# A decoder step on one core: rows of 320 floats for the normed inputs and the gate*up outputs, placed by address

## The chip, the core and the metric

The kernel runs on one core of a Trainium2 chip. The metric is device time in microseconds for one execution. Three executions of the kernel before took 1245.39 to 1247.6 us, with a median of 1246.92 us.

The core has five engines, each with its own queue, and they meet only at semaphores: PE (TensorE, matrix products), DVE (VectorE), ACT (ScalarE), POOL (GpSimd) and SP (SyncE, which here only issues DMAs). Tiles lie in SBUF, which has 128 partitions; a tile takes the same range of byte addresses in each of them. PE writes its sums into PSUM. A matrix product is two instructions on PE: LDWEIGHTS (PEld in the profile) reads the stationary operand from SBUF, and MATMUL (PE in the profile) streams the moving operand from SBUF past it.

## The reference

One inference step of a two-layer decoder for 256 prompt tokens and 8 times 4 sample tokens, 288 tokens in all, with a model width of 1024 and an FFN width of 2816. Each layer is a mixer between two half-step SwiGLU FFNs; the mixer of layer 0 is a short gated convolution, that of layer 1 a sparse attention with three branches.

```
xp = xp + 0.5 * swiglu(rmsnorm(xp, norm_ffa[i]), w_ffa_gu[i], w_ffa_down[i])
...
xp = xp + 0.5 * swiglu(rmsnorm(xp, norm_ffb[i]), w_ffb_gu[i], w_ffb_down[i])

def swiglu(x, w_gu, w_down):
    g, u = jnp.split(x @ w_gu, 2, axis=-1)
    return (jax.nn.silu(g) * u) @ w_down
```

The four FFNs, the projections into and out of the convolution and those into and out of the attention are products of the 288 tokens with some 170 MB of weights in float32. These products are what the change touches.

## The kernel before

All activations lie turned: 128 channels on the partitions, the 288 tokens along the free axis. The normed input of a layer is eight such rows (KD = 8), the gated hidden values of half an FFN are ten or twelve.

**Three products for one.** The float32 products run in a fast format with fewer bits (float32r). So that nothing is lost, both operands are split into a high and a low part, and three of the four cross products are summed in PSUM: high by high, low by high, high by low. For the weights, `Weights.high` (L223) writes `whi` by a copy on ACT and `Weights.low` (L245) writes `wlo` by a subtraction on DVE, each 128 x 1024 floats from a `raw` tile that a DMA has filled; there are four buffers of each. For the activations the pairs are `xh`, `xl` (the normed input, written by `gated_hi` and `gated_lo`) and `Ah`, `Al` (the gated values, written at L552 and L553 in `ffn` and in `parts` of `conv_mixer`).

**The stream on PE.** `product` (L467) goes over the rows k and issues, for each, three matmuls through `mm` (L303): `ah[k]` past `hi[k]`, `al[k]` past `hi[k]`, `ah[k]` past `lo[k]`. The stationary operand is 128 columns of 4 bytes, so 512 bytes in each partition; the moving operand is one row of 288 floats, 1152 bytes. Every matmul has a LDWEIGHTS of its own, also where the weights are those of the matmul ahead. While one matmul streams, PE already loads the weights of the next: beside `ah[k]` past `hi[k]` runs the load of `hi[k]` again, beside `al[k]` past `hi[k]` that of `lo[k]`, and beside `ah[k]` past `lo[k]` that of `hi[k+1]`. `products2` (L476) does the same for two outputs at once. There are 7800 such matmuls.

**The rows.** `xh` and `xl` are tiles of 8 x 288 floats in a pool that lives through the whole kernel; `attention_out` (L1513) replaces them, for the rest of layer 1, by a second pair of the same names in another pool. `Ah` and `Al` are tiles of 12 x 288 floats, made by `pair` (L526). A row of 288 floats is 1152 bytes, four and a half times 256, so every second row starts 128 bytes further on modulo 256. `product` takes its operands from these tiles by index and knows no addresses. In the built program the tiles start, modulo 256 bytes, at

| tile | row k even | row k odd | distance to the weights' start, modulo 256 |
|---|---|---|---|
| `whi`, `wlo` (each of the 8 pieces of 512 bytes) | 224 | 224 | |
| `xh`, `xl`, first pair | 64 | 192 | 96 and 224 |
| `xh`, `xl`, second pair (from `attention_out` on) | 0 | 128 | 32 and 160 |
| `Ah`, `Al` | 0 | 128 | 32 and 160 |

**Order.** The source order sets the order on each engine outside the attention; inside it a planner (`Plan`) does. Weights come in through SP's queue in chunks of up to 1 MB into four `raw` buffers, and are split two units ahead of their use.

Of the kernel before, what the change touches and what calls it, by code (L numbers as in the profile page):

```python
# [9 lines left out]
F32R = mybir.dt.float32r  # L10
# [6 lines left out]
P = 128  # L17
D = 1024
KD = D // P
# [6 lines left out]
N = NP + NS  # L26
# [39 lines left out]
EARLY = ("POOL", "DVE", "DVE")  # L66

V_FFA, V_PE, V_MIX, V_FFB, V_FIN, V_CONV = 0, 16, 32, 48, 64, 72


def weight_chunks():
# [200 lines left out]
def tile_step(ctx, tc, x_turned, vectors, state_turned, cmp_pages, sel_pages, cache_win, win_pages, page_table,  # L272
# [4 lines left out]
    const = ctx.enter_context(tc.tile_pool(name="const", bufs=1))  # L277
# [15 lines left out]
    def mmb():  # L293
        return bank("mm")
# [7 lines left out]
    def mm(out, lhsT, rhs, start, stop):  # L302
        nc.tensor.matmul(out, lhsT, rhs, start=start, stop=stop, skip_group_check=True)  # L303
# [3 lines left out]
    work = ctx.enter_context(ExitStack())  # L307
# [64 lines left out]
    for _ in range(4):  # L372
        c = W.chunk()
# [4 lines left out]
    plan_ffn()  # L378


    xh = const.tile([P, KD, N], F32R, name="xh")
    xl = const.tile([P, KD, N], F32R, name="xl")
    ss = const.tile([P, N], F32, name="ss")
    normed = [xh, xl]

# [20 lines left out]
    def gated(d, v):  # L406

        gated_hi(d, v)
        gated_lo(d, v)
        squares(d)  # L410
# [56 lines left out]
    def product(p, ah, al, k0, nk, start, stop, lower=None):  # L467
        hi, lo = W.next(lower)
        o = p[:hi.shape[2], :N]
        for k in range(nk):  # L470
            s, e = start and k == 0, stop and k == nk - 1
            mm(o, hi[:, k], ah[:, k0 + k], s, False)
            mm(o, hi[:, k], al[:, k0 + k], False, False)
            mm(o, lo[:, k], ah[:, k0 + k], False, e)
# [18 lines left out]
    def tick(cost):  # L493

        due = [w for w in waiting if w[0] <= 1]
        waiting[:] = [w for w in waiting if w[0] > 1]
        for w in waiting:
            w[0] -= 1
        for _, f in due:
            f()  # L500
        fill.step(cost, 0 if fill.hold else 1)
# [22 lines left out]
    fill = Fill()  # L524

    def pair(work, name, n):  # L526
        return (work.tile([P, n, N], F32R, name=name + "h", bufs=1), work.tile([P, n, N], F32R, name=name + "l", bufs=1))

    def passing(d):

# [4 lines left out]

    def ffn(work, after, begin=None):
        Ah, Al = pair(work, "A", 12)
        factor = []

# [48 lines left out]

    def conv_mixer(work, v_next):
        Ah, Al = pair(work, "A", 12)  # L590
        ust = work.tile([P, KD, 18], F32, name="ust", bufs=1)
        rB = None
# [919 lines left out]

    def attention_out(work, v_next):  # L1513

        normed[:] = pair(work, "x", KD)
        ps = [mmb(), mmb()]
        us = [W.next(), W.next()]
        for n, (part, x) in enumerate(((0, xh), (0, xl), (1, xh))):
            for p, u in zip(ps, us):
                for k in range(KD):  # L1520
                    mm(p[:, :N], u[part][:, k], x[:, k], n == 0 and k == 0, n == 2 and k == KD - 1)
        for d in range(KD):
            if d < 2:
                p = ps[d]
            else:
                p = mmb()
                product(p, xh, xl, 0, KD, True, True)
            nc.vector.tensor_add(xT[:, d], p[:, :N], xT[:, d])
            gated(d, v_next)
            tick(3.0)  # L1530
# [20 lines left out]
    with psum_banks(mm=4, tr=2, acc=2), tc.tile_pool(name="ffn1", bufs=2) as work:  # L1551
        attention_out(work, V_FFB + KD)
        for b in range(NB):
            later(1 + 4 * b, lambda b=b: nc.gpsimd.dma_start(win_s[b], cache_win[0, b, NT:]))
        ffn(work, lambda d: last(work, d))
        final_out(work)
# [57 lines left out]
```

## Time and profile before

| | |
|---|---|
| median of three runs | 1246.92 us (1245.39 to 1247.6) |
| profiled execution, its own time | 1246.98 us |
| span of its trace, first to last instruction | 1245.2 us |
| granted TensorE clock, mean | 0.998 |
| MATMULs in the trace | 10047, of which 7800 are the split products |
| busy: PE, DVE, ACT, POOL | 99%, 58%, 46%, 19% of the span |
| DMA | 262 MB, mean 210 GB/s |

Times are microseconds from the first instruction unless marked ns. A group of instructions is a line of kernel.py with an engine, an operation and the names of its tiles, `mm<-xh,whi` being a product of `xh` and `whi` into PSUM tile `mm`. MATMULs overlap in the trace: the recorded time of one runs from its start to the modelled end of its results, so it is longer than the distance from one start to the next. That distance is called the **step** below. It is read from the chain that ended last, which gives the start, the length and the count of an unbroken run of matmuls: length by count is the mean step.

### The profile page before, as it was taken

Reading aid. Unit: us, or ns where it says so; the run is one execution under the profiler, and the core shown is the slowest. Engines: PE = TensorE matmul, PEld = TensorE weight load, DVE = VectorE, ACT = ScalarE, POOL = GpSimd, SP = SyncE. Lnnn points to the kernel's source line nnn. Section 1 sums busy time; section 2 is a strip of 40 time slices with the busy share of each in tenths; the row PEclk is TensorE's granted clock in tenths of the full one; section 3 lists DMA queues with packets and bytes.
Section 4 is the critical chain, followed back from the end, with each engine's and each line's share of the span. In section 5 each row is a group of like instructions: output and inputs, shape, how many; then the busy total and the mean of one; then the engine's idle time right before and its main releaser. Section 6 shows DMA issues by size and latency. Waiting matters only on the chain.

```text
span 1245.2 us, 25757 instructions
## 1 busy us (share of the span) xinstructions
PE 1227.8 (99%) x10047; PEld 1162.6 (93%) x10047; DVE 726.3 (58%) x1363; ACT 571.2 (46%) x1011; POOL 241.2 (19%) x237
## 2 busy tenths in 40 slices
PE   9999999999999999999999999999999999999997
PEld 8999999999999999999899999999866699999997
DVE  6663555666765545556564455677568566654554
ACT  6443344533544334335343344544377655433444
POOL 0260121221322201212120012130022222200211
PEclk9999999999999999999999999999999999999999
DMA  7764655756566466546563453496699857565422
GB/s 278 257 216 173 236 171 185 254 186 218 189 213 211 155 206 233 198 151 232 197 237 117 176 174 115 165 339 219 232 362 331 291 209 302 191 249 203 165 101 78
DMA packets 89066, 262.00 MB, mean 210 GB/s; under 512 B 9937, under 2 KB 43090, under 8 KB 73714
## 3 DMA queue, kind: packets, MB, share of 16 engines
q1 hardware_dynamic: 87922, 249.66, 57.0%
q0 software_dynamic: 256, 8.32, 1.7%
q10 hardware_dynamic: 768, 2.38, 0.5%
q8 instruction: 79, 1.29, 0.4%
q14 instruction: 41, 0.34, 0.1%
HBM read 257.31 MB, written 11.35 MB: 216 GB/s over the span
## 4 chain that ended last, share of the span: by engine, by line
PE 91%; DVE 3%; ACT 3%; DMA 2%; issue 1%; SPq 0%; POOL 0%; DVEq 0%; ACTq 0%
PE mm L303 82%; PE tr L303 5%; PE acc L303 3%; PE tr L334 1%; DMA early<-in_sel_pages_dram 1%; DVE wlo L247 1%; ACT S L1211 1%; DMA raw<-in_w_nsa_out_dram 0%; SPq L1008 0%; ACT L534 0%; ACT whi L238 0%; DMA wlo<-in_sel_pages_dram 0%; DMA raw<-in_w_ffa_gu_dram 0%; DVE xT L583 0%; ACT S L1367 0%
## 5 line engine op out<-in xcount | busy, mean ns | idle before, releaser
L303 PE MATMUL mm<-xh,whi 128*128 128x288 f32 x1832 | 543.3, 298 | 3.0 <-DVE xl L1476 1.1
L303 PE MATMUL mm<-xh,wlo 128*128 128x288 f32 x1832 | 539.9, 297 | 0.0
L303 PE MATMUL mm<-xl,whi 128*128 128x288 f32 x1832 | 532.8, 293 | 0.0
L247 DVE TENSOR_TENSOR wlo<-raw,whi 128x1024 fp32r<-128x1024 f32 (+2 forms) x361 | 407.8, 1143 | 94.3 <-ACT whi L238 91.5
L238 ACT ACTIVATE whi<-raw 128x1024 fp32r<-128x1024 f32 (+2 forms) x365 | 343.3, 952 | 100.3 <-PE mm L303 92.9
L303 PEld LDWEIGHTS mm<-xh,whi 128*128 128x128 f32 x1832 | 342.9, 188 | 8.8 <-issue 4.2
L303 PEld LDWEIGHTS mm<-xl,whi 128*128 128x128 f32 x1832 | 346.8, 190 | 0.3
L303 PEld LDWEIGHTS mm<-xh,wlo 128*128 128x128 f32 x1832 | 341.8, 187 | 0.6 <-DVE wlo L247 0.4
L303 PE MATMUL mm<-Ah,wlo 128*128 128x288 f32 x768 | 228.6, 298 | 1.0 <-DVE wlo L247 0.9
L303 PE MATMUL mm<-Ah,whi 128*128 128x288 f32 x768 | 227.9, 297 | 0.0
L303 PE MATMUL mm<-Al,whi 128*128 128x288 f32 x768 | 227.2, 296 | 0.0
L549 POOL TENSOR_TENSOR a<-s,t 128x288 f32<-128x288 f32 x80 | 110.3, 1379 | 517.8 <-DVE t L547 405.5
L303 PEld LDWEIGHTS mm<-Ah,wlo 128*128 128x128 f32 x768 | 144.2, 188 | 2.3 <-DVE wlo L247 2.1
L303 PEld LDWEIGHTS mm<-Ah,whi 128*128 128x128 f32 x768 | 145.0, 189 | 0.6 <-issue 0.4
L303 PEld LDWEIGHTS mm<-Al,whi 128*128 128x128 f32 x768 | 144.6, 188 | 0.0
L552 ACT ACTIVATE Ah<-a 128x288 fp32r<-128x288 f32 x88 | 39.1, 445 | 163.4 <-POOL a L549 150.1
L545 ACT ACTIVATE s<-t 128x288 f32<-128x288 f32 x88 | 39.1, 445 | 156.4 <-DVE t L543 156.3
L547 DVE TENSOR_TENSOR t<-mm,rB 128x288 f32<-128x288 f32 x88 | 40.2, 457 | 115.1 <-PE mm L303 115.1
L583 DVE SCALAR_TENSOR_TENSOR xT<-mm,xT 128x288 f32<-128x288 f32 x64 | 29.2, 456 | 90.1 <-PE mm L303 89.9
L553 DVE TENSOR_TENSOR Al<-a,Ah 128x288 fp32r<-128x288 f32 x88 | 40.8, 463 | 65.9 <-ACT Ah L552 65.9
L303 PE MATMUL tr<-cp,W 128*64 128x256 f32 x512 | 58.8, 382 | 0.0
L387 ACT ACTIVATE xh<-xT,vecT 128x288 fp32r<-128x288 f32 x48 | 25.2, 534 | 62.0 <-DVE xT L583 41.1
(283 smaller groups left out, 847.1 us busy)
## 6 DMA issues: line engine op xcount, KB each, us to landing
raw<-in_w_ffb_gu_dram SPq DMA_DIRECT2D x44, 1024.0 KB, 5.2
raw<-in_w_ffa_gu_dram SPq DMA_DIRECT2D x42, 1024.0 KB, 5.3
cp<-in_cmp_pages_dram SPq DMA_DIRECT2D x256, 128.0 KB, 4.3
early<-in_sel_pages_dram SPq DMA_DIRECT2D x56, 256.0 KB, 5.8
raw<-in_w_ffa_down_dram SPq DMA_DIRECT2D x16, 768.0 KB, 4.5
raw<-in_w_conv_in_dram SPq DMA_DIRECT2D x12, 1024.0 KB, 5.1
raw<-in_w_ffb_down_dram SPq DMA_DIRECT2D x16, 768.0 KB, 5.9
raw<-in_sel_pages_dram SPq DMA_DIRECT2D x48, 256.0 KB, 5.0
```

What stands on the lines that cost most here:

```text
L238: self.nc.scalar.activation(parts[0], v, AF.Copy)
L247: (lower or self.nc.vector).tensor_sub(parts[1], v, parts[0])
L303: nc.tensor.matmul(out, lhsT, rhs, start=start, stop=stop, skip_group_check=True)
L334: nc.tensor.transpose(out, in_, ident[:k, :k])
L387: nc.scalar.activation(normed[0][:, d], xT[:, d], AF.Copy, scale=vecT[:, v + d:v + d + 1])
L545: nc.scalar.activation(s1, t1, AF.Silu)
L547: nc.vector.tensor_mul(t2, pu[:, :N], rB)
L549: (nc.vector if last else nc.gpsimd).tensor_mul(a, s1, t2)
L552: nc.scalar.activation(Ah[:, f], a, AF.Copy)
L553: nc.vector.tensor_sub(Al[:, f], a, Ah[:, f])
L583: nc.vector.scalar_tensor_tensor(xT[:, d], py[:, :N], 0.5, xT[:, d], op0=OP.mult, op1=OP.add)
L1211: nc.scalar.activation(o, o, AF.Exp, scale=-1.0, bias=x, accum_out=e)
```

## The change

The two tiles of a pair are now made by a new function `rows`. A row takes 320 floats (1280 bytes, five times 256), of which the first 288 are used, so that all rows of a tile start at the same address modulo 256. `SKIP` leaves 0, 16 or 56 floats free ahead of the first row, and `BEHIND` leaves some free behind the last, so that whatever lies next starts where it should. The second pair of normed inputs is now called `zh`, `zl`, so that `SKIP` can treat it on its own.

```
+ROW = 320
+SKIP = dict(xh=0, xl=16, Ah=56, Al=16, zh=56, zl=16)
+BEHIND = dict(xl=8, zl=56)

-    xh = const.tile([P, KD, N], F32R, name="xh")
-    xl = const.tile([P, KD, N], F32R, name="xl")
+    def rows(pool, name, n, **k):
+
+        t = pool.tile([P, SKIP[name] + n * ROW + BEHIND.get(name, 0)], F32R, name=name, **k)
+        return t[:, SKIP[name]:][:, :n * ROW].rearrange("p (n c) -> p n c", c=ROW)[:, :, :N]
+
+    xh, xl = rows(const, "xh", KD), rows(const, "xl", KD)

     def pair(work, name, n):
-        return (work.tile([P, n, N], F32R, name=name + "h", bufs=1), work.tile([P, n, N], F32R, name=name + "l", bufs=1))
+        return [rows(work, name + part, n, bufs=1) for part in "hl"]

-        normed[:] = pair(work, "x", KD)
+        normed[:] = pair(work, "z", KD)
```

No instruction is added, removed or moved: on all five engines the rows of operations, tiles and shapes are the same as before, one for one, apart from the new names. What differs is addresses. In the built program of the change they are, modulo 256 bytes:

| tile | every row | distance to the weights' start, modulo 256 |
|---|---|---|
| `whi`, `wlo` (each of the 8 pieces) | 64 | |
| `xh`, `Ah`, `zh` (high parts) | 64 | 0 |
| `xl`, `Al`, `zl` (low parts) | 128 | 64 |

`raw` moves from 224 to 64 as well. The highest address in use rises from 227136 to 229280 bytes in each partition.

## The prediction

> **What bounds the kernel now.** I read the page's list of busy times first, then its chain and its costliest groups.
>
> ```profile
> PE 1227.8 (99%) x10047; PEld 1162.6 (93%) x10047; DVE 726.3 (58%) x1363; ACT 571.2 (46%) x1011; POOL 241.2 (19%) x237
> PE 91%; DVE 3%; ACT 3%; DMA 2%; issue 1%; SPq 0%; POOL 0%; DVEq 0%; ACTq 0%
> L303 PE MATMUL mm<-xh,whi 128*128 128x288 f32 x1832 | 543.3, 298 | 3.0 <-DVE xl L1476 1.1
> L303 PE MATMUL mm<-xh,wlo 128*128 128x288 f32 x1832 | 539.9, 297 | 0.0
> L303 PE MATMUL mm<-xl,whi 128*128 128x288 f32 x1832 | 532.8, 293 | 0.0
> ...
> L303 PE MATMUL mm<-Ah,wlo 128*128 128x288 f32 x768 | 228.6, 298 | 1.0 <-DVE wlo L247 0.9
> L303 PE MATMUL mm<-Ah,whi 128*128 128x288 f32 x768 | 227.9, 297 | 0.0
> L303 PE MATMUL mm<-Al,whi 128*128 128x288 f32 x768 | 227.2, 296 | 0.0
> ```
>
> PE carries the end, and of PE the six groups of split products: 3 x 1832 + 3 x 768 = 7800 matmuls. They wait for next to nothing (3.0 and 1.0 us in all). So the question is how far apart their starts are. The mean over a group (298, 297, 293 ns) is not that distance, since matmuls overlap, but differences between groups count: a matmul that streams longer is recorded longer. The step itself stands in the chain in order of time, asked for in three windows: one within the first FFN's gate and up products, one within the down products that follow, and one within the last FFN's gate and up products.
>
> ```profile
> 39.90 45.22 PE mm L303 x342
> ...
> 111.92 16.13 PE mm L303 x121
> ...
> 1139.94 60.13 PE mm L303 x451
> ```
>
> The columns are start, length and count. The steps are 45.22/342 = 132.2 ns, 16.13/121 = 133.3 ns and 60.13/451 = 133.3 ns. The first and the third window run the same code on operands of the same shape: `xh`, `xl` past `whi`, `wlo`. They differ in where the rows lie, 96 and 224 bytes from the weights modulo 256 in the first, 32 and 160 in the third. `Ah`, `Al` in the second window lie like those of the third, and have its step. So **addresses do move the step**, by 1.1 ns between the two placements that the trace holds.
>
> How low could the step go? Two rows from the timeline give the pace of a stream without hindrance: the compression products of the cached pages, whose moving rows are 256 columns.
>
> ```profile
> 107.78 3.67 PE L303 MATMUL tr<-cp,W 128*64 128x256 f32 x32
> ...
> 108.05 3.41 PE L303 MATMUL tr<-cp,W 128*64 128x256 f32 x30
> ...
> L303 PE MATMUL tr<-cp,W 128*64 128x256 f32 x26 | 3.0, 379 | 0.0
> ```
>
> Both rows end at the same time, so thirty instructions, issued in 15 pairs, take 3.41 us less the 0.38 us of the last one: 3.03 us for 14 pairs, 216 ns a pair, 108 ns for 256 columns. For 288 columns that makes 121.5 ns. The split products take 11 to 12 ns more than this for each matmul.
>
> **The terms.** Of the 5496 matmuls on normed inputs, 8 x 24 in `attention_out` and 22 x 2 x 24 in the last FFN, 1248 in all, are on the second pair; 4248 have the step of the first window and 1248 + 2304 = 3552 that of the others: 4248 x 132.2 + 3552 x 133.3 = 1035 us of the 1245.2 us span, a mean of 132.7 ns. Every nanosecond in the step is worth 7.8 us.
>
> *Removed:* the alternation of rows by 128 bytes, and the odd distances: before, all were 32 bytes off a multiple of 64 from the weights; now they are 0 for the high and 64 for the low rows. *Added:* no instruction. ACT and DVE write the rows with the same shapes and whole within each row; they stand idle for much of the time beside PE (46% and 58% busy), which would hide a few ns in a write. If it did not, it would show where PE waits for them, 0.8 us for `xh` and 0.6 us for `xT` now:
>
> ```profile
> PE mm L303 <- DVE wlo L247: 0.9, 4, 0.3
> ...
> PE mm L303 <- ACT xh L387: 0.8, 1, 0.8
> ...
> PE mm L303 <- DVE xT L583: 0.6, 1, 0.6
> ...
> ACT whi L238 <- PE mm L303: 92.9, 61, 5.4
> ```
>
> The last row says who is late next if PE gets faster: nobody soon. ACT waits 92.9 us for PE to free weight buffers, more than any gain considered here. If that cover were gone, each weight unit would show up like the four waits for `wlo`, some 0.2 us each. The float32 products of the attention and the compression change addresses too (`raw` moves); I cost them at nothing, since the compression already paces at its columns, and no row tells what an address does to the attention's; bounded by the spread between placements above, 1.1 ns in 133, or 0.8%, of the page's 1245.2 - 1035 = 210 us left, that is 1.7 us either way.
>
> *What the distance costs or saves* no row shows, since no distance that is a multiple of 64 occurs in this trace. Bounds: below, the unhindered 121.5 ns, 11.2 ns less, 7800 x 11.2 = 87 us. Above, the spread that the trace has between the slow and the quick groups, put on once more (under the rivals). For a value between, I take what the matmuls themselves show. The quickest group is `xl` past `whi`, 293 ns; its neighbours in the same stream have 297 and 298. The weight loads beside them tell the same:
>
> ```profile
> L303 PEld LDWEIGHTS mm<-xl,whi 128*128 128x128 f32 x1824 | 345.8, 190 | 0.3
> L303 PEld LDWEIGHTS mm<-xh,whi 128*128 128x128 f32 x1824 | 341.9, 188 | 8.7 <-issue 4.2 <-ACT xh L387 1.5 <-DVE xl L1476 1.2
> L303 PEld LDWEIGHTS mm<-xh,wlo 128*128 128x128 f32 x1824 | 340.8, 188 | 0.5 <-DVE wlo L247 0.4
> ```
>
> The load listed as `xl,whi` runs beside the matmul `xh,whi`: the slowest load (190 ns) stands beside the slowest matmul (298 ns). I read this as both streams reaching for the same part of SBUF at once. If every matmul came down to the quickest group's 293 ns, that saves 1832 x (5 + 4 + 0) + 768 x (5 + 4 + 3) ns = 16.5 + 9.2 = 25.7 us, a step of 129.4 ns. Against the profiled execution's own 1246.98 us (a span of 1245.2 and 1.8 us around it, and 0.06 us above the median, so no correction) that gives 1221.3 us. This value is nearer the rows on this shape than the 121.5 ns of another, so I take it: **1221 us**.
>
> A rule speaks against any gain. The Trainium skill, page "TensorE: Matmul & The Clock Gate", section "Step-by-step: what each phase is for", gives PE two independent read ports into SBUF and says that loading the next weights takes no read bandwidth from the running matmul. By that, distances to the weights would not matter and the time would stay at 1247 us; the same page's "Back-to-back issue gap" (columns / 2.4 + 2.5 ns) would have the step at an estimated 122.5 ns already. This trace, with 132.2 and 133.3 ns for one shape at two placements, agrees with neither as it stands.
>
> **The rivals.**
>
> *The stream itself is slow.* Then the 132 ns are the pace of this format at 288 columns, whatever is loaded beside it. A matmul that ran alone speaks for it:
>
> ```profile
> 18.33 0.19 PEld L303 LDWEIGHTS mm<-xl,whi 128*128 128x128 f32 x1
> 18.46 0.29 PE L303 MATMUL mm<-xl,whi 128*128 128x288 f32 x1
> ...
> 18.68 0.19 PEld L303 LDWEIGHTS mm<-xh,wlo 128*128 128x128 f32 x1 [0.15 <-DVE wlo L247]
> 18.68 0.40 PE L303 MATMUL mm<-xh,wlo 128*128 128x288 f32 x1
> ```
>
> Between 18.46 and 18.68 no load started, since `wlo` was late, and yet the matmul is recorded at 0.29 us, like those with a load beside them. Against it: the 1.1 ns between placements. It gives 1247 us, or, where the second pair and `Ah`, `Al` reach the step of the first, 3552 x 1.1 = 3.9 us less, 1243 us. The rule above is this rival's strong form.
>
> *The hindrance goes entirely.* The step falls to near the unhindered pace: 1247 - 87 = 1160 us. For it: that the slack of 11 ns is there and nothing else on PE explains it. Against it: the matmul alone.
>
> *High rows and weights start in step.* A distance of 0 means that the matmul and the load that start together begin at the same address modulo 256. If two reads of the same part of SBUF collide, this is the worst distance, not the best. It holds for two matmuls of three (both on the high rows, beside which `whi` is loaded). Priced by the spread in the trace, 5 ns (298 against 293): 7800 x 2/3 x 5 = 26 us, 1273 us; if only the pair with the same piece of `whi` collides, 7800 / 3 x 5 = 13 us, 1260 us. It decides as soon as the high groups' mean passes 298 ns. For it: the slowest load stands beside the slowest matmul already. Against it: the matmul reads 1152 bytes in the time in which the load reads 512, so that the two part at once, whatever their start.
>
> *That the change does not do what it says* is out: the built program has the addresses of the table.
>
> **How the numbers follow.** The forecast, anything between 1180 and 1244 us: 0.58. Hindrance gone, below 1180: 0.07. Stream slow, within 0.2% of 1246.92 us (1244.4 to 1249.4; about what a measurement of this kernel can tell from no change): 0.15. In step, slower: 0.20, of which some 0.08 up to 1258 us. The range 1180 to 1258 leaves out 0.07 below and 0.12 above. Faster 0.65, same 0.15, slower 0.20.
>
> **What would show it.** Right: the same three windows of the chain give one step, since all rows now lie alike, near 129 ns; the groups of `xh` and `xl` draw together near 293 ns; the loads come to 187 or 188 ns each; the waits on PE stay as they are. If the windows stay at 132 or 133 ns, the stream is slow by itself. If the high groups pass 298 ns and the low ones do not, the start in step costs. Wrong in another way: a step that falls while the span does not, with new waits of PE for `wlo` or for DMA; then something else is late, which the 92.9 us above speak against.

## The result, and the profile after

The change takes **1235.99 us** (median of 4 runs, 1234.79 to 1236.77), the kernel before on the same chip 1247.26 us (1245.39 to 1250.07): a ratio of **0.9907, interval 0.9886 to 0.9928**. The 25.7 us forecast are 11.3 us. In a later comparison (`a2_change` below) it was 0.9908, interval 0.9893 to 0.9922.

From the page after, the busy times, the chain's shares and the groups that answer to those of before:

```profile
PE 1218.2 (99%) x10047; PEld 1153.3 (93%) x10047; DVE 730.3 (59%) x1363; ACT 571.1 (46%) x1011; POOL 236.8 (19%) x237
...
PE 92%; ACT 3%; DVE 3%; DMA 2%; issue 1%; POOL 0%; SPq 0%; DVEq 0%; ACTq 0%
...
L307 PE MATMUL mm<-xh,whi 128*128 128x288 f32 (+1 forms) x1480 | 436.5, 297 | 2.5 <-DVE xl L1484 1.1
L307 PE MATMUL mm<-xl,whi 128*128 128x288 f32 (+1 forms) x1480 | 432.4, 294 | 0.0
L307 PE MATMUL mm<-xh,wlo 128*128 128x288 f32 (+1 forms) x1480 | 428.7, 292 | 0.0
...
L307 PE MATMUL mm<-Ah,whi 128*128 128x288 f32 x768 | 226.4, 295 | 0.0
```

PE is still the bound, busy for 9.6 us less (1227.8 to 1218.2), but its groups have not moved as forecast (the groups before also held the second pair, which is now listed apart as `zh`, `zl`): `xh,wlo` lost 5 ns (297 to 292), `xh,whi` 1 ns (298 to 297), and `xl,whi`, the quickest before, is slower (293 to 294). The three windows of the chain in order of time (start, length, count):

```profile
39.94 45.10 PE mm L307 x344
...
111.89 15.21 PE mm L307 x116
...
1129.96 60.04 PE mm L307 x458
```

All three are now 131.1 ns a matmul (45.10/344, 15.21/116, 60.04/458), where before they were 132.2, 133.3 and 133.3. And the waits, first of PE, then of ACT for weight buffers (total us, times, longest):

```profile
PE mm L307 <- DVE wlo L251: 1.1, 4, 0.3
...
PE mm L307 <- DVE xT L591: 0.6, 1, 0.6
...
ACT whi L242 <- PE mm L307: 86.1, 58, 5.3
```

Nothing new is late: PE waits four times for `wlo` as before, and ACT has still 86.1 us in hand of its 92.9. The whole gain is the step's. One thing in this profile is not the change's doing: for 3.4 us behind the attention the granted clock was 0.50 (the third last column below), and the matmuls there start 240 ns apart. In the same three microseconds the clock was 1.00 in the profile before, and in that of `a2_change`, the same kernel once more.

```profile
989.00:992.00 3.00, 3.00 (x15) 3.00 (x14) 3.00 (x3) 2.00 (x2) 0.77 (x1) 0.50 0.98 396
```

### The profile page after: what moved, and what is told of

It is laid out like the page before. It is cut to its first block, busy times and chain, and to the rows that moved or that the text cites. A ratio compares the mean times of both kernels' runs of the same rounds, so it can differ in the third digit from the quotient of the medians.

```text
span 1235.0 us, 25757 instructions
## 1 busy us (share of the span) xinstructions
PE 1218.2 (99%) x10047; PEld 1153.3 (93%) x10047; DVE 730.3 (59%) x1363; ACT 571.1 (46%) x1011; POOL 236.8 (19%) x237
## 4 chain that ended last, share of the span: by engine, by line
PE 92%; ACT 3%; DVE 3%; DMA 2%; issue 1%; POOL 0%; SPq 0%; DVEq 0%; ACTq 0%
PE mm L307 83%; PE tr L307 5%; PE acc L307 3%; PE tr L338 1%; DMA early<-in_sel_pages_dram 1%; ACT S L1219 1%; DVE wlo L251 1%; DMA raw<-in_w_nsa_out_dram 0%; ACT L542 0%; ACT whi L242 0%; DMA raw<-in_w_ffa_gu_dram 0%; DVE xT L591 0%; ACT S L1375 0%; DVE S L1371 0%; ACT sq L404 0%
## 5 line engine op out<-in xcount | busy, mean ns | idle before, releaser
L307 PE MATMUL mm<-xh,whi 128*128 128x288 f32 (+1 forms) x1480 | 436.5, 297 | 2.5 <-DVE xl L1484 1.1
L307 PE MATMUL mm<-xl,whi 128*128 128x288 f32 (+1 forms) x1480 | 432.4, 294 | 0.0
L307 PE MATMUL mm<-xh,wlo 128*128 128x288 f32 (+1 forms) x1480 | 428.7, 292 | 0.0
L242 ACT ACTIVATE whi<-raw 128x1024 fp32r<-128x1024 f32 (+2 forms) x365 | 343.2, 952 | 97.5 <-PE mm L307 86.1
L307 PEld LDWEIGHTS mm<-xh,whi 128*128 128x128 f32 (+1 forms) x1480 | 276.8, 188 | 7.9 <-issue 3.8
L307 PEld LDWEIGHTS mm<-xl,whi 128*128 128x128 f32 (+1 forms) x1480 | 277.0, 188 | 0.5 <-DVE xl L398 0.2
L307 PEld LDWEIGHTS mm<-xh,wlo 128*128 128x128 f32 (+1 forms) x1480 | 276.0, 187 | 0.4 <-DVE wlo L251 0.2
L557 POOL TENSOR_TENSOR a<-s,t 128x288 f32<-128x288 f32 x80 | 104.8, 1310 | 514.9 <-DVE t L555 376.4
L307 PE MATMUL mm<-zh,whi 128*128 128x288 f32 x352 | 103.5, 294 | 0.0
L307 PE MATMUL mm<-zl,whi 128*128 128x288 f32 x352 | 103.3, 294 | 0.0
L307 PE MATMUL mm<-zh,wlo 128*128 128x288 f32 x352 | 102.8, 292 | 0.0
L591 DVE SCALAR_TENSOR_TENSOR xT<-mm,xT 128x288 f32<-128x288 f32 x64 | 29.2, 456 | 86.1 <-PE mm L307 85.6
```

The lines of the kernel that those rows point to most:

```text
L242: self.nc.scalar.activation(parts[0], v, AF.Copy)
L557: (nc.vector if last else nc.gpsimd).tensor_mul(a, s1, t2)
L591: nc.vector.scalar_tensor_tensor(xT[:, d], py[:, :N], 0.5, xT[:, d], op0=OP.mult, op1=OP.add)
```

## The experiments

All times of the split products below are **steps**, start to start. Since they turn out to lie on a grid, they are given in cycles too, a cycle being 1/2.4 ns. That is half of what one more column costs a plain float32 product in `m5_loads_fp32`: 215.8 ns at 256 columns and 242.5 at 288 make 0.833 ns a column. The mean granted clock was 0.990 in `m1_bench` and 0.996 to 0.999 in the others; where a step fell into a stretch at 0.50, the text says so. The bench runs (`m1` to `m5`) are the changed kernel, and behind its end a program on PE that repeats the triple of `product` on a tile of its own, with nothing beside it on the other engines once the tile is filled:

```
for r in range(reps):
    for k in range(KD):
        a, b = (B[:, x + k * step:x + k * step + n] for x in (xh_, xl_))
        u, v = (B[:, x + k * P:x + k * P + cols] for x in (hi, lo))
        mm(o, u, a, True, True)
        mm(o, u, b, True, True)
        mm(o, v, a, True, True)
```

Weights lie in pieces of 512 bytes as in the kernel, rows 320 floats apart unless said, and the distances of high and low rows to the weights modulo 256 bytes are set one by one ("0/64" is the change's). Each setting runs 72 matmuls, of which the last 48 give the step (where several starts are compared, 48 matmuls a start, of which the last 24).

**Which distances matter? `m1_bench`.**

> The changed kernel with a bench behind its end: 91 settings of 72 split-product matmuls each (high row past high weights, low row past high weights, high row past low weights), on idle data, with nothing else running. It adds work and no output depends on it. Settings: 8 x 8 distances of high and low rows from the weights in steps of 32 bytes at rows of 320 floats; rows of 288 floats at 8 equal distances; all addresses shifted together; low weights shifted alone; loads of 32, 64, 96 columns; rows of 64 to 512 columns. Theory A (distance to the weights counts): shifting all together changes nothing, the 64 settings spread by at least 2 ns, and 0/64 is among the lowest, 131.1 ns. Theory B (the stream itself is slow, some 29 array cycles, 10 to 12 ns, over columns at any distance): loads of 32 columns bring the step down by less than 2 ns; the 64 settings spread little. Theory C (a cost for each matmul against a slower rate): a fixed cost gives columns x 0.417 ns plus about 11 ns at every width from 320 to 512; a slower rate gives 131.1/288 = 0.455 ns a column, 233 ns at 512. Rows of 288 at distance 32 give 133.3 ns, at 96 132.2 ns, if the bench shows what the kernel does.

Measured, in ns (down: distance of the low rows, across: of the high rows, in bytes):

```
low\high    0     32     64     96    128    160    192    224
  0      131.8  133.2  132.6  131.1  131.0  132.2  132.2  132.8
 32      131.7  133.3  131.1  133.3  133.3  131.9  131.1  133.3
 64      131.3  133.3  131.7  132.2  132.8  131.9  132.6  132.2
 96      132.7  134.4  133.3  131.7  131.1  133.9  132.2  133.3
128      132.2  133.3  132.2  131.1  133.3  134.4  133.4  133.4
160      131.1  133.3  133.3  133.3  132.2  133.3  131.1  133.3
192      134.4  135.6  133.3  132.2  132.6  133.3  133.3  132.2
224      131.1  132.2  132.9  133.3  133.3  132.2  132.2  133.3
```

Distances move the step between 131.0 and 135.6 ns, and most entries repeat a few values, 314.67, 317.33, 320, 322.67 or 325.33 cycles: 944 to 976 cycles for three matmuls, in steps of 8. The change's 0/64 gives 131.3 ns, and rows of 288 floats at the distances of the kernel before gave its own 133.3 (320.0 cycles at 32) and 132.2 (317.3 at 96): the bench reproduces both kernels, so DVE, ACT and DMA at work beside PE have no part in the step. Weights and rows shifted together by 32, 64, 128 or 192 bytes gave 314.4 to 316.4 cycles, no wider than 0/64 spreads by itself from start to start (313.9 to 317.2 in `m4_starts`). So distances count and absolute addresses do not, and the forecast's 129.4 ns stands nowhere in the table. Neither theory of the width held alone: 144.4 ns at 320 columns is what a fixed cost gives (though `m2_bench` had 147.2), 232.0 ns at 512 is nearly the 233 of a slower rate.

**One part of the change at a time: `e1_rows288`, `e2_off32`, `e3_low0`.** Rows of 288 floats again, in places that keep the new first distances (even rows 0 and 64, odd rows 128 and 192):

```
-ROW = 320
+ROW = 288
```

> The change with rows of 288 floats again, the offsets kept: high rows lie 0 and 128, low rows 64 and 192 bytes from the weights modulo 256, all still multiples of 64. Theory A1 (being off a multiple of 64 costs): the step stays at 131.1 ns, 1236 us. Theory A2 (the alternation of rows costs, each 128 bytes on being a change of distance): back to 132 to 133 ns, 1243 to 1247 us.

All rows alike, but 32 and 96 bytes from the weights:

```
-SKIP = dict(xh=0, xl=16, Ah=56, Al=16, zh=56, zl=16)
-BEHIND = dict(xl=8, zl=56)
+SKIP = dict(xh=0, xl=16, Ah=0, Al=16, zh=0, zl=16)
+BEHIND = dict(xl=0, zl=48)
```

> The change with rows of 320 floats, but all moved rows 32 bytes further from the weights: 32 for the high rows, 96 for the low. Theory A1 (off a multiple of 64 costs): 132 to 133.3 ns, 1243 to 1247 us. Theory A2 (only the alternation costs): 131.1 ns, 1236 us. Stream theory: between 131 and 132.5 ns whatever is done.

High and low rows both at distance 0:

```
+SKIP = dict(xh=0, xl=0, Ah=56, Al=0, zh=56, zl=0)
+BEHIND = dict(xl=24, zl=8)
```

> The change with low rows at distance 0 as the high ones, instead of 64. If a start in step with the weights costs, all three matmuls of a row pay now instead of two: above 131.1 ns, 132 or more, over 1243 us. If only the jump from one row to the next counts, the jumps are 128, 128 and 128 bytes modulo 256 instead of 192, 64 and 128, and the step returns to 133.3 ns as in the old placement at 32. If neither, 131.1 ns and 1236 us.

The first and second window of the chain for `e1_rows288`:

```profile
39.95 45.09 PE mm L307 x341
...
111.92 15.21 PE mm L307 x115
```

the first and third for `e2_off32`:

```profile
39.90 45.17 PE mm L307 x336
...
1129.90 60.10 PE mm L307 x447
```

and the first and third for `e3_low0`:

```profile
39.98 45.03 PE mm L307 x342
...
1129.92 60.17 PE mm L307 x457
```

| run | distances high / low | step, ns | time, us | ratio to before (1247.11) |
|---|---|---|---|---|
| `e1_rows288` | 0, 128 / 64, 192 | 132.2 | 1243.41 | 0.9963 [0.9949, 0.9977] |
| `e2_off32` | 32 / 96 | 134.4 | 1259.53 | 1.0099 [1.0075, 1.0123] |
| `e3_low0` | 0 / 0 | 131.7 | 1240.25 | 0.9934 [0.9914, 0.9954] |

Both parts of the change are needed for the whole gain. With the old row length two thirds of the gain go (1243.41 against 1235.99 us). Equal rows 32 bytes off are worse than the kernel before, and 23.5 us worse than the change; no theory had foreseen more than 133.3 ns there. The 131.7 ns of `e3_low0` lie between its expectations, 131.1 ns and 132 or more. The times follow the step: between `e1_rows288` and `e2_off32` 16.1 us for 2.2 ns, 7.3 us a ns, beside the 7.8 of the prediction. The rule of the Trainium skill weighed in the prediction (the two read ports) has no place for those 16 us, which two placements of the same instructions make. The groups of `e2_off32`:

```profile
L307 PE MATMUL mm<-xh,whi 128*128 128x288 f32 (+1 forms) x1480 | 439.1, 299 | 2.1 <-DVE xl L1484 1.0
L307 PE MATMUL mm<-xh,wlo 128*128 128x288 f32 (+1 forms) x1480 | 437.1, 298 | 0.0
L307 PE MATMUL mm<-xl,whi 128*128 128x288 f32 (+1 forms) x1480 | 435.8, 296 | 0.0
```

Against the change's 297, 292 and 294, all three are recorded longer, the one on `wlo` most. (How far such means can be read as prices is taken up under the prediction.)

**The fine map, and what else moves the step: `m2_bench`, `m3_bench`.** The same loop at distances in steps of 16 bytes; weights alone shifted; fewer weight columns; other widths; and two-byte operands.

> The bench again, added behind the changed kernel: 192 more distances (steps of 16 bytes), loads of 32, 64, 128 columns at the two slow settings 32/96 and 0/192, the weights alone shifted at fixed rows, the low weights alone shifted at 32/96, widths of 256 to 320 columns in steps of 8, and the same loop on two-byte operands. Collision with the load: at 32/96 a load of 32 columns (a quarter of the bytes) costs clearly less than one of 128 (134.4 ns): 132 ns or less; and shifting the weights alone moves the step as the distances say. Rows alone: the step stays at 134.4 ns with a load of 32 columns, and shifting the weights alone leaves 131.1 ns. Stream theory: four-byte rows are what costs the 11 ns: on two-byte operands the step falls to 120 to 123 ns at every distance. If a finer offset could free the stream, some of the 192 lies below 131 ns; if 131.1 ns (944 array cycles for three matmuls) is the stream's floor, none does.

Of the 256 distances of both maps, 69 give 131.3 ns or less, but only two less than 131.0: 130.0 ns (312 cycles) at 112/240 and at 144/192. The median is 132.2 ns and the worst 135.6. (The entry 16/0, first in `m2_bench`, comes out at 142.3 ns only because the granted clock was still 0.50 at its beginning; its last 24 matmuls give 132.2.) So the kernel before sat near the middle of the map, and the change at its usual lower edge. With the weights alone shifted past fixed rows the step moved between 131.0 and 134.5 ns, in seven of eight places to what the map has for the distances that result, within 0.4 ns. Smaller loads beside the same rows helped the slow setting: at 32/96 the step was 134.4 ns with loads of 128 columns, 131.1 with 64 and 132.2 with 32. Two-byte operands, from the chain within their stretch:

```profile
3371.99 30.14 PE mm L307 x246
```

That is 122.5 ns (294 cycles) for the same 288 columns, at all four distances tried. Hence the 131 ns belong to float32r, and two-byte rows felt none of these four distances. (The Trainium skill, page "TensorE: Matmul & The Clock Gate", section "Back-to-back issue gap", gives columns / 2.4 + 2.5 ns: its 122.5 ns hold for two bytes to the tenth, and miss this format by 8.6.)

> The bench with the three matmuls of a row in other orders (high past high, high past low weights, low past high weights; low row ahead; and an order turned round at every second row, so that equal rows follow each other), each at the 64 distances; then one and the same row throughout, past high or past low weights. If the jump between successive rows decides, other orders change the map and their best may lie below 131.1 ns, and the same row throughout has one step at any distance. If the distance to the weights that are loaded beside decides, the map changes with the order as well, but the same row throughout still moves with its distance. If 131.1 ns is the stream's floor, no order gets below it.

Two of the three other orders gave the same map in the main (58 and 61 of 64 entries within 0.3 ns of `m1_bench`); in both, as in the kernel, two high rows and one low row follow each other in turn. The third, turned round at every second row, changes that sequence, and kept only 20 of 64 entries. So beside the distances the sequence of the rows counts. None of the orders gave less than 131.0 ns. With one and the same row for all three products there is no jump between them. Past high weights this ran at distance 0 alone, eight times over, with 131.7 ns each time. Past low weights the row was moved in steps of 32 bytes: 131.7 ns at 0 and at 96 bytes, 132.2 at 64, 133.3 at the other five. A distance moves the step with no jump between rows as well.

**Is a quicker placement worth it? `m4_starts`, `f1_112_240`, `f2_144_192`, `a2_change`.** The first repeats settings from 16 starts each, with a matmul of 256 to 376 columns ahead to shift the phase:

> The bench with each setting entered from 16 different starts (one matmul of 256 to 376 columns ahead of it), 48 matmuls each, the last 24 counted. If a setting has one step of its own, all 16 agree. If the rhythm in which loads and matmuls fall in with each other depends on how it begins, one setting shows several steps, each a multiple of 8 array cycles for three matmuls (936, 944, 952, 960 and so on, that is 130.0, 131.1, 132.2, 133.3 ns). Expected: 0/64 at 131.1 ns from nearly all starts; 112/240 and 144/192, at 130.0 ns once in the run before, at 130.0 ns from some starts only; 0/192 split between 131.1 and 134.4 ns, as the two runs before had it. Loads of 32 and 64 columns: at 131.1 to 132.2 ns at every distance, if the load's bytes are what collides.

```
distance   cycles a matmul, 16 starts
0/64       313.9 to 317.2, mean 315.0
0/0        316.0 in 16
144/192    312.0 in 16
112/240    312.0 in 9, 325.3 in 7
0/192      314.7 in 4, 322.7 in 12
32/96      322.7 in 16
```

Some distances have **two steps**, and which one a stream gets depends on how it starts. That is why single entries of the map are not to be trusted. The same run had loads of 32 and 64 columns, expected at 131.1 to 132.2 ns at every distance. They gave 131.1 and some 132.0 ns at 0/64, 132.2 and 131.1 at 32/96, 131.1 and 130.0 at 0/0, and at 112/240 **128.9** (309.3 cycles, from all 16 starts) and 131.1. The chain within one start at 112/240 with loads of 32 columns:

```profile
2701.95 5.16 PE mm L307 x40
```

The kernels, each with a column offset `IN` within the row of 320 floats (`[:, :, IN[name]:IN[name] + N]` in `rows`), and the change again as `a2_change`.

For `f1_112_240`, A and z at 112/240, x left at 0/64:

```
+SKIP = dict(xh=0, xl=16, Ah=0, Al=20, zh=0, zl=20)
+BEHIND = dict(xl=8, zl=44)
+IN = dict(xh=0, xl=0, Ah=20, Al=32, zh=20, zl=32)
```

For `f2_144_192`, all at 144/192:

```
+SKIP = dict(xh=0, xl=0, Ah=0, Al=8, zh=0, zl=8)
+BEHIND = dict(zl=56)
+IN = dict(xh=12, xl=24, Ah=28, Al=32, zh=28, zl=32)
```

> The change with the gated values and the second pair of normed inputs at 112 and 240 bytes from the weights, the first pair left at 0 and 64. If 130.0 ns is that setting's own step, 3360 matmuls gain 1.1 ns each, 3.7 us: 1232 us. If it was a rhythm met by chance, 131.1 ns or more there and 1236 us or above.

> The change with high rows at 144 and low rows at 192 bytes from the weights throughout. If 130.0 ns is that setting's own step: 7800 x 1.1 ns = 8.6 us less than the change, 1227 us. If it was met by chance: 131.1 ns or more, 1236 us or above.

> The changed kernel itself once more, beside the other two on the same chip: 131.1 ns and 1236 us, 0.9% below the kernel before.

| run | time, us | ratio to before (1247.17) |
|---|---|---|
| `a2_change` | 1234.69 | 0.9908 [0.9893, 0.9922] |
| `f1_112_240` | 1239.84 | 0.9946 [0.9931, 0.9961] |
| `f2_144_192` | **1228.10** | **0.9855 [0.9841, 0.9870]** |

`f2_144_192` beats both kernels, with 130.0 ns wherever the chain was read:

```profile
39.93 45.11 PE mm L308 x347
...
111.97 15.08 PE mm L308 x116
...
1140.00 45.11 PE mm L308 x347
```

`f1_112_240`, expected to gain too, lost to the change. Its chain, in two down products, `Ah`, `Al` at the same addresses in both:

```profile
111.93 15.08 PE mm L308 x116
...
199.95 15.06 PE mm L308 x111
```

130.0 ns in the one, 135.7 ns in the other: the two steps that 16 starts had shown, now within one kernel.

**What is left of 131 ns when the load is all but taken away? `m5_loads_fp32`.** The same loop with loads of 4, 16 and 128 columns, then as plain float32, eight starts each.

> After the kernel's end a bench runs the triple of split products with loads of 4, 16 and 128 columns at the distances 0/64, 32/96, 112/240 and 144/192, and then the same rows as plain float32 (each product is then two passes on PE) with loads of 64 and 128 columns; eight starts each, 48 products a start, the step taken from the last 24. Output is the kernel's. If the loads are what holds the step above one column a cycle, loads of 4 columns bring it from 131 ns to 122 or 123 ns at every distance, and the distances stop to matter. If the stream of four-byte rows is slow by itself, loads of 4 columns leave it at 129 to 132 ns. If four-byte rows in general are slow, the passes of plain float32 take 129 to 132 ns as well; if it is the split products' format alone, they take 121 to 123 ns, as the 108 ns for 256 columns of the compression say.

```
distance    4 columns       16 columns      128 columns   (cycles a matmul)
0/64        314.7           314.7           313.8 to 317.1
32/96       314.7           316.0           322.7
112/240     314.7           314.7           312.0 or 325.4
144/192     314.7           314.2 to 315.3  312.0
```

The chain within one start at 32/96, with loads of 4 columns and of 128:

```profile
1410.46 6.16 PE mm L307 x47
...
1509.94 3.36 PE mm L307 x25
```

The step is 131.1 ns with next to nothing loaded, at all four distances, and 134.4 ns with full loads at this one. The load beside it does hinder the stream, but by 3.3 ns here and by next to nothing at the change's distances. **With hardly a load the stream takes 131.1 ns**, and the change has reached that. It is no floor: full loads at 144/192 give 130.0 ns, and loads of 32 columns at 112/240 gave 128.9. So the load beside a stream shifts its step both ways. Plain float32 showed what my "unhindered" pace was. One stretch of 256 columns past weights of 64, like the compression's, from the chain:

```profile
3489.82 15.32 PE mm L307 x71
```

One instruction after the other, 215.8 ns each. In the compression two instructions start within 7 ns of each other, for products that `kernel.py` writes to the two halves of the output's partitions, and the pair takes 216 ns: they run **side by side**, each at 215.8 ns.

## Why the prediction was right and wrong

**What bounds it, the direction, and the reading that addresses move the step: right.** PE carries the end before and after, no wait of PE grew by more than 0.2 us, the three windows fell to one step, the loads came to 188 and 187 ns, and ACT's cover held:

```profile
L307 PEld LDWEIGHTS mm<-xh,whi 128*128 128x128 f32 (+1 forms) x1480 | 276.8, 188 | 7.9 <-issue 3.8
L307 PEld LDWEIGHTS mm<-xl,whi 128*128 128x128 f32 (+1 forms) x1480 | 277.0, 188 | 0.5 <-DVE xl L398 0.2
L307 PEld LDWEIGHTS mm<-xh,wlo 128*128 128x128 f32 (+1 forms) x1480 | 276.0, 187 | 0.4 <-DVE wlo L251 0.2
```

The price of a nanosecond was right as well: the prediction's own counts give 4248 x 1.1 + 3552 x 2.2 = 12.5 us, and 11.3 were measured. Between the two profiled spans it is 10.2 us, since 3.4 us of the later one ran at half the clock; the profiled span of `a2_change`, with a clock of 1.00 there, is 1232.7 us, 12.5 less than before. The float32 products that the prediction put at nothing stayed there as far as the runs show: plain float32 took the same time at all four distances of `m5_loads_fp32`. (`attention_out`'s products read the first pair, not the second, as the prediction counted them: 192 matmuls and 0.2 us.)

**The mis-sized term** is "if every matmul came down to the quickest group's 293 ns, that saves ... 25.7 us, a step of 129.4 ns". Measured: a step of 131.1 ns, less than half of it. The inference failed, not the sum. The recorded means of three matmuls that follow each other are not three separate prices. Their average less the step is 296 - 132.5 = 163.5 ns before (132.5 being the step of the normed inputs alone, by the prediction's counts) and 294.3 - 131.1 = 163.2 ns after: the average follows the step, and a single group's mean says how the three share it out. The starts in the traces say the same: on the first pair `xh,whi`, `xl,whi` and `xh,wlo` take 134.5, 129.3 and 133.0 ns on average to the next start before, and 131.4, 132.0 and 130.4 after. `xl,whi` at 293 was quick beside slow neighbours, not free of hindrance, and rose to 294 when the others fell.

**The bound below it failed first.** The 121.5 ns were read from the compression's pairs, as two passes one after the other of 108 ns each. `m5_loads_fp32` shows them as two instructions side by side at 215.8 ns. With 11 ns of slack on the table, 3.3 looked modest. Down to the step with hardly a load it was 132.7 - 131.1 = 1.6 ns, and the change took all of it; down to the best kernel here, `f2_144_192`, it was 2.7.

**The rivals.** *The stream itself is slow* was right in its main point, that most of the 132 ns are there whatever is loaded, and got 0.15: the lone matmul at 18.46 us that was recorded like its neighbours was the best witness in the trace, and loads of 4 columns bear it out (131.1 ns). Its time was not right, since 1.6 ns hung on the loads after all. *The hindrance goes entirely* is, as a mechanism, close to what happened at the change's distances, where full loads and loads of 4 columns give the same step to 0.3 ns; its 1160 us rested on the 121.5 ns. *High rows and weights start in step* falls: with high and low rows at distance 0, 1240.25 us, faster than before, 4.3 us over the change and nowhere near 1260.

**What stays open:** why float32r streams 288 columns in 314.7 cycles rather than 294, why the steps lie on a grid of 8 cycles for three matmuls, by what the load shifts the step (a collision on reading SBUF was the prediction's reading; no run shows it), and why some loads make the stream quicker than loads of 4 columns do: 1.1 ns at 144/192 with full loads, 2.2 at 112/240 with loads of 32. The runs show that they are so, not why. A matmul without any load between was not tried; 4 columns was the least.

## What to carry to other kernels

Before a gain is priced by the quickest member of a pipelined stream, or by another stream's pace, take the step of the whole group, see whether two instructions of the yardstick start together, and find the pace with the suspect taken away: one bench with loads of 4 columns would have put the step to hope for near 131 ns rather than 121.5. In a kernel bound by float32r products with full weight loads, place moving rows by their distance to the weights modulo 256 bytes, alike for every row (131.1 to 134.4 ns between placements here, 23.5 us in 1236). Measure a placement from several starts, since some have two steps, and look up the granted clock in the very stretch that a step is read from.

## What the runs showed of the hardware that was not expected

- Steps of float32r products with full loads mostly lie on a grid of 8 cycles for three matmuls: 936, 944, 952, 960, 968, 976 (203 of the 256 entries of the map to within 1 cycle of the three).
- One placement can hold two steps: 112/240 gave 130.0 or 135.6 ns by its start.
- Smaller loads are not always the better ones: at 112/240 the step was 131.1 ns with loads of 4, 16 and 64 columns, and 128.9 with 32.
- The pace of float32r by width, at 0/64 with rows 512 floats apart (`m1_bench`): some 112 ns at 64 columns and 111.7 at 192, 117.8 at 256, 144.4 at 320 (147.2 in `m2_bench`), 232.0 at 512, all at a granted clock of 1.00. With full loads 64 columns cost as much as 192, and the cycles over one a column grow from 26.7 at 256 to 44.8 at 512.
- The granted clock fell to 0.50 in the midst of that series, from the end of the 64 columns on, and the step there rose from 112 to 213 ns. The 128 columns, whose 213.3 ns thus say nothing of full clock, ran wholly within this stretch (granted clock in the third last column):

```profile
2031.00:2054.00 23.00, 23.00 (x110) 23.00 (x110) 0.00 (x0) 0.00 (x0) 0.00 (x0) 0.50 0.00 1
```

- Plain float32 products took 582 cycles an instruction for 288 columns and 518 for 256, 6 over two a column, the former at all four distances; two-byte ones 6 over one a column. Of these formats only float32r felt where its rows lie.
